# A hybrid diffusion block on one core: a hand-written scan order with its stores issued later and its loads earlier

## The chip, the cores and the metric

The kernel runs on one core of a Trainium2 chip. The metric is the device time of one execution in microseconds. "Before" is the kernel without the change. All line numbers are those of the kernel before. A few words used throughout: PE is TensorE, DVE is VectorE, ACT is ScalarE, POOL is GpSimd, and SP is SyncE, which computes nothing here and issues almost all transfers. Each engine takes its instructions in the order in which they were written for it.

## The reference, cut to what matters

One layer over 2048 latent tokens and 256 context tokens, width 1024, in float32. After a projection, branch A is a gated delta rule that runs over the sequence in both directions and branch B is a gated short convolution; both are projected, gated and merged, multiplied by one more matrix, and added to the input under a layer norm. The change touches the scan of branch A and what is run beside it. Its core is this loop over chunks:

```
def step(s, xs):
    qk_i, q_dec_i, k_dec_i, u_i, w_i, d_i = xs
    v_new = u_i - jnp.einsum('bhck,bhkv->bhcv', w_i, s)
    o = jnp.einsum('bhck,bhkv->bhcv', q_dec_i, s) + jnp.einsum('bhcs,bhsv->bhcv', qk_i, v_new)
    s = s * d_i[..., None, None] + jnp.einsum('bhck,bhcv->bhkv', k_dec_i, v_new)
    return s, o
```

It is run for two directions over the same chunks, and the two outputs are added, then normalised per head and multiplied by a gate:

```
o = o * lax.rsqrt(jnp.mean(o * o, axis=-1, keepdims=True) + RMS_EPS) * w
y = o * jax.nn.silu(z)
merged = jax.nn.sigmoid(g_a) * (y_a @ w_a) + jax.nn.sigmoid(g_b) * (y_b @ w_b)
```

## The kernel before

Three stages follow one another. The projections fill the first half of the time. Then comes the scan (method `window`), and at the end the output product and the layer norm (method `final`). The change lies in the scan and in its helpers.

The scan works in chunks of 128 tokens with all 8 heads in one tile. There are 18 chunks (2 of context, 16 latent) and two directions, so 36 **visits**; forward and backward alternate. Visits 0 to 3 are context. A latent chunk is visited twice, once in each direction. The second visit is marked `again`; visits 20 to 35 are of that kind. A first visit computes two products of keys and queries (`N` and `QK`, method `gram`), multiplies them by the decays and keeps the raw products in HBM. A visit that is `again` loads them from there (`gram_load`, L153) and only multiplies (L160). A first visit stores its output (`od`); an `again` visit loads it (`op`, L1311), adds its own (L1320), normalises the sum (`norm`), and turns and gates it (`norm_out`: load `zat`, transpose on PE, multiply on DVE at L1494, store `yad` at L1495).

The loop is a software pipeline written out by hand: `tc.manual_schedule` keeps the written order on all five engines. Pass `i` of the loop works on four visits at once: `v0` (visit i) updates the state, `v1` inverts its triangular matrix, `v2` forms `QK`, `v3` loads its keys and decays, forms `N` and begins its inverse. The inverse of `v3` is a generator `sol` of 20 small DVE steps (L186 to L215), handed out one or two at a time between the other work by `go(sol, n)`. The decays of `v3` are a generator `dec` of four parts (`visit_decay`). The norm of the visit before is a generator `norms` of five parts.

Beside the scan runs filler work on PE: `dense(n)` takes the next n matmuls of the eight remaining products (jobs b1, b2, b0, b3, then a0 to a3; each job is 8 units `m` of 24 matmuls). Each unit loads its two weight tiles `wh`, `wl` one unit ahead (L361, two buffers), loads a gate tile `gt`, and ends in `evac`: DVE multiplies (L1227), in the a jobs POOL adds `mt` (L1229), and SP stores (L1230). An a job may begin when its four chunks have been normalised (`ready`, `done`); its input `yr` is loaded (L1205) and split by ACT and POOL (L366, L367).

What matters for the change is the one list of transfers that SP goes through in the written order. A store waits there until its data are ready, and all loads written after it wait behind it. Four such places:

- `evac` issues its store right behind the multiplication (L1230);
- `norm_out` issues, for each half of the heads, the load of `zat` (L1490) and then the store of the product (L1495), so that the second load stands behind the first store;
- the kept product `QK` of `v2` is loaded (L1367 calls L153) in the pass in which it is used, a few lines above its use;
- `kT` and the decays `gcb` of `v3` are loaded at the start of the pass in which `visit_decay` begins to work on them; `kT` has three buffers, and the fourth visit's load waits for the product of `v0` with its keys (L320).

Of the kernel before, what the change touches and what calls it, by code (L numbers as in the profile page):

```python
# [15 lines left out]
P = 128  # L16
D = 1024
KT = 8
H = 8
# [18 lines left out]
class Kern:  # L38
    def __init__(self, tc):
        self.tc = tc  # L40
        self.nc = tc.nc
        self.es = ExitStack()
        self.due, self.tick, self.phase_of, self.pending, self.tail = [], 0, {}, [], False

# [52 lines left out]
    def visit_load(self, v):  # L97

        nc, g2 = self.nc, self.g2
        src = v["src"]  # L100
        v["kT"] = self.gk.tile([P, H, P], F32, name="kT", bufs=3)
        nc.sync.dma_start(v["kT"], src["kT"])
        v["gcb"] = self.gb.tile([P, H, P], F32, name="gcb")
        nc.sync.dma_start(v["gcb"].rearrange("p h t -> p (h t)"), src["gc"])
# [15 lines left out]
    def visit_decay(self, v):  # L120
# [20 lines left out]
        for h in range(H):  # L141
            nc.vector.scalar_tensor_tensor(out=gcb[:, h, :], in0=gcb[:, h, :], scalar=gcT[:, h:h + 1], in1=self.mask[d],
                                           op0=ALU.subtract, op1=ALU.min)
        nc.scalar.activation(out=gcb, in_=gcb, func=AF.Exp)
# [1044 lines left out]
    def window(self, es, settle):  # L1189
# [36 lines left out]
        def evac(job, m, ps, gt, mt):  # L1226
            nc.vector.scalar_tensor_tensor(out=gt, in0=gt, scalar=1.0, in1=ps, op0=ALU.add, op1=ALU.mult)  # L1227
            if job[0] == "a":
                (nc.vector if self.tail else nc.gpsimd).tensor_tensor(out=gt, in0=gt, in1=mt, op=ALU.add)  # L1229
            nc.sync.dma_start((self.mb_d if job[0] == "b" else self.mg_d)[job[1]][m], gt)  # L1230
# [15 lines left out]
        def fillers():  # L1246
# [3 lines left out]
            for jn, job in enumerate(jobs):  # L1250
# [17 lines left out]
                for m in range(8):  # L1268
# [3 lines left out]
                    if m < 7:  # L1272
                        w.append(self.load_w(W, m + 1))
                    elif nxt is not None and ready(nxt):
                        fed = True
                        w.append(self.load_w("w_b" if nxt[0] == "b" else "w_a", 0))
                        if nxt[0] == "a":
                            for k in range(KT):
                                fetch(nxt, k)
# [61 lines left out]
        with tc.manual_schedule(engines={ET.PE, ET.DVE, ET.Activation, ET.Pool, ET.SP}):  # L1341
# [6 lines left out]
            def turn():  # L1348
                for n, parts in turned:
                    self.norm_out(n, parts)  # L1350
                    done.add(n)
                turned.clear()

            for i in range(-3, nv):
                get = lambda k: vs[i + k] if 0 <= i + k < nv else None
                v0, v1, v2, v3 = get(0), get(1), get(2), get(3)
                dec = self.visit_decay(v3) if v3 else iter(())
                if i < -1:
# [5 lines left out]
                if v3:  # L1364
                    self.visit_load(v3)
                    self.gram_load(v3, "N")
                if v2 and v2["latent"]:  # L1367
                    self.gram_load(v2, "QK")
# [10 lines left out]
                if v3:  # L1379
                    self.visit_load_q(v3)  # L1380
                go(sol, 2)
                if v1:
                    self.inv_d16(v1)
                go(sol)
# [8 lines left out]
                if i >= -1:  # L1393
                    dense(4)
                go(sol, 2)
# [9 lines left out]
                if v0:  # L1405
                    self.st_o(v0, 1)
                if late:
# [7 lines left out]
                if v0:  # L1415
                    self.st_u(v0, 1)
                if v1:
                    self.inv_d32(v1)
                go(dec)
                go(norms)  # L1420
                go(sol, 9)
# [13 lines left out]
                if i == -1 or v3 and v3["again"] or not v3:  # L1435
                    dense(8)
                if v1:
# [5 lines left out]
                go(sol)  # L1443
            go(norms, 9)
            turn()
            return fil
# [15 lines left out]
    def norm(self, n, parts):  # L1462
# [3 lines left out]
        ms = g2.tile([P, H], F32, name="ms")  # L1466
        for hs, o in parts:
# [15 lines left out]
    def norm_out(self, n, parts):  # L1483
# [4 lines left out]
        for hs, o in parts:  # L1488
            za = g1.tile([P, 4, P], F32, name="zat", bufs=2)
            nc.sync.dma_start(za, self.za_d[n // 4][n % 4][:, hs, :])  # L1490
# [4 lines left out]
            nc.sync.dma_start(self.ya_d[gi][hs, :, sl].rearrange("h p t -> p h t"), za)  # L1495
# [225 lines left out]
```

## Time and profile before

| | |
|---|---|
| time, median of 2 runs | 3618.56 us (3615.84 to 3621.28) |
| profiled execution, its own time | 3615.66 us |
| its span, first to last instruction | 3613.9 us |
| busy, share of the span | PE 84%, DVE 62%, ACT 42%, POOL 39% |
| PE clock granted, mean | 0.910 of full speed |
| projections | 0 to 1855 us |
| scan, start (passes -3 to 0) | 1855 to 1967 us |
| scan, first visits (passes 1 to 17) | 1967 to 2473 us |
| scan, passes 18 to 34 | 2473 to 3238 us |
| last pass and norms | 3238 to 3297 us |
| rest of the fillers, output product, layer norm | 3297 to 3614 us |

Read it so: PE is the busiest engine over the whole span, but the whole span is a mean over stages that have different limits. 17 passes with first visits take 506 us; the 17 passes after them, in which a visit is `again`, take 765 us.

### The profile page before, as it was taken

Reading aid. Unit: us, or ns where it says so; the run is one execution under the profiler, and the core shown is the slowest. Engines: PE = TensorE matmul, PEld = TensorE weight load, DVE = VectorE, ACT = ScalarE, POOL = GpSimd, SP = SyncE. Lnnn points to the kernel's source line nnn. Section 1 sums busy time; section 2 is a strip of 40 time slices with the busy share of each in tenths; the row PEclk is TensorE's granted clock in tenths of the full one; section 3 lists DMA queues with packets and bytes.
Section 4 is the critical chain, followed back from the end, with each engine's and each line's share of the span. In section 5 each row is a group of like instructions: output and inputs, shape, how many; then the busy total and the mean of one; then the engine's idle time right before and its main releaser. Section 6 shows DMA issues by size and latency. Waiting matters only on the chain. (4 is left out here: it accounts for less than half of the span.)

```text
span 3613.9 us, 60210 instructions
## 1 busy us (share of the span) xinstructions
PE 3033.2 (84%) x22089; PEld 2499.0 (69%) x22089; DVE 2237.2 (62%) x5658; ACT 1516.8 (42%) x3405; POOL 1395.4 (39%) x1021
## 2 busy tenths in 40 slices
PE   7899899999989999999977888887665555577788
PEld 4677688888867778887865777776554545465576
DVE  7657555556566656564226777876665555544499
ACT  4654543334465543333413555554443334332121
POOL 3544467666665546666610111111102112103264
PEclk9999999999999999999988898998877777788899
DMA  5535753235643322233355556566444444356742
GB/s 202 142 95 153 220 161 105 77 117 172 193 143 111 95 66 83 83 97 113 101 176 211 182 194 240 199 225 227 148 155 170 176 152 160 129 174 219 244 155 105
DMA packets 405380, 557.23 MB, mean 154 GB/s; under 512 B 28244, under 2 KB 278613, under 8 KB 404060
## 3 DMA queue, kind: packets, MB, share of 16 engines
q1 hardware_dynamic: 382158, 520.77, 44.1%
q10 hardware_dynamic: 22926, 32.62, 2.5%
q8 instruction: 173, 2.83, 0.3%
q14 instruction: 123, 1.01, 0.1%
HBM read 391.66 MB, written 161.64 MB: 153 GB/s over the span
## 5 line engine op out<-in xcount | busy, mean ns | idle before, releaser
L783 PE MATMUL pd<-bh,ah 128*128 128x512 f32 x2240 | 892.9, 399 | 10.4 <-ACT u L803 5.8
L785 PE MATMUL pd<-bh,al 128*128 128x512 f32 x2240 | 880.2, 393 | 0.0
L784 PE MATMUL pd<-bl,ah 128*128 128x512 f32 x2240 | 880.0, 393 | 0.0
L367 POOL TENSOR_TENSOR al<-s,ah 128x512 fp32r<-128x512 f32 x348 | 479.0, 1380 | 470.0 <-ACT ah L366 447.0
L367 POOL TENSOR_TENSOR al<-raw,ah 128x512 fp32r<-128x512 f32 x260 | 370.2, 1428 | 320.7 <-ACT ah L366 285.2
L783 PEld LDWEIGHTS pd<-bh,ah 128*128 128x128 f32 x2240 | 425.2, 190 | 98.9 <-issue 6.5
L785 PEld LDWEIGHTS pd<-bh,al 128*128 128x128 f32 x2240 | 424.8, 190 | 90.5 <-POOL al L367 0.3
L784 PEld LDWEIGHTS pd<-bl,ah 128*128 128x128 f32 x2240 | 425.4, 190 | 85.2
L118 POOL TENSOR_TENSOR kt<-kt,kd 128x1024 f32<-128x1024 f32 x36 | 68.4, 1901 | 842.9 <-DMA kt<-kd 574.2
L366 ACT CAST ah<-s 128x512 fp32r<-128x512 f32 x352 | 214.1, 618 | 292.4 <-PE pd L784 268.5
L366 ACT CAST ah<-raw 128x512 fp32r<-128x512 f32 x264 | 162.3, 616 | 260.7 <-PE pd L784 169.4
L1282 PE MATMUL pf<-ah,wh 128*128 128x512 f32 x512 | 227.1, 444 | 49.3 <-DMA wh<-w_bhd 17.2
L340 PE MATMUL pst<-S,qd 128*128 128x128 f32 x512 | 122.1, 327 | 151.3 <-DVE ot L1320 139.4
L769 DVE TENSOR_TENSOR s<-s,raw 128x512 f32<-128x512 f32 x80 | 110.7, 1383 | 220.0 <-POOL s L769 220.0
L1286 PE MATMUL pf<-ah,wl 128*128 128x512 f32 x512 | 230.2, 450 | 18.2 <-DMA wl<-w_ald 16.7
L1284 PE MATMUL pf<-al,wh 128*128 128x512 f32 x512 | 223.7, 437 | 2.7 <-POOL al L367 2.6
L340 PEld LDWEIGHTS pst<-S,qd 128*128 128x128 f32 x512 | 97.4, 232 | 157.4 <-DVE ot L1320 141.5
L208 DVE TENSOR_TENSOR R<-R,rb 128x120 f32<-128x120 f32 (+4 forms) x540 | 189.3, 350 | 1.2
L205 DVE TENSOR_TENSOR rb<-rb,R 128x120 f32<-128x120 f32 (+4 forms) x540 | 166.8, 309 | 14.2
L1282 PEld LDWEIGHTS pf<-ah,wh 128*128 128x128 f32 x512 | 110.0, 215 | 74.0 <-issue 30.4
L146 POOL TENSOR_TENSOR qd<-qd,qT 128x1024 f32<-128x1024 f32 x32 | 75.6, 2363 | 215.0 <-ACT qd L138 128.2
L308 PE MATMUL pinv<-r,w 64*64 64x64 f32 x576 | 57.2, 272 | 113.2 <-ACT w L297 113.2
(349 smaller groups left out, 6011.6 us busy)
## 6 DMA issues: line engine op xcount, KB each, us to landing
raw<-in_w_in SPq DMA_DIRECT2D x160, 512.0 KB
kT<-kTd SPq DMA_DIRECT2D x36, 512.0 KB
gcb<-gcd SPq DMA_DIRECT2D x36, 512.0 KB
kt<-kd SPq DMA_DIRECT2D x36, 512.0 KB
vh<-vd SPq DMA_DIRECT2D x36, 512.0 KB
wh<-w_bhd SPq DMA_DIRECT2D x32, 512.0 KB
wl<-w_bld SPq DMA_DIRECT2D x32, 512.0 KB
qT<-qTd SPq DMA_DIRECT2D x32, 512.0 KB
```

The costliest lines, as they stand in the source:

```text
L205: nc.vector.tensor_tensor(out=t, in0=t, in1=bc(R[:, :, j:j + 1], c.stop - c.start), op=ALU.mult)
L208: nc.vector.tensor_tensor(out=R[:, :, c], in0=R[:, :, c], in1=t, op=ALU.add)
L340: nc.tensor.matmul(po[:, j, :], v["qd"][:, h, :], S[:, h, :], start=True, stop=False)
L366: self.nc.scalar.copy(out=hi, in_=src)
L367: (eng or self.nc.gpsimd).tensor_tensor(out=lo, in0=src, in1=hi.bitcast(F32), op=ALU.subtract)
L769: eng.tensor_tensor(out=o, in0=a, in1=b, op=op)
L783: mm(ps, hi[:, k, :], bh, start=(first and k == 0), stop=False, skip_group_check=not first)
L784: mm(ps, hi[:, k, :], bl, start=False, stop=False, skip_group_check=not first)
L785: mm(ps, lo[:, k, :], bh, start=False, stop=(last and k == 3), skip_group_check=not first)
L1282: mm(ps, wh[:, k, :], ah, start=(k == 0), stop=False)
L1284: mm(ps, wh[:, k, :], al, start=False, stop=False)
L1286: mm(ps, wl[:, k, :], ah, start=False, stop=(k == KT - 1))
```

## The change

1. **Stores behind their data.** `evac` and `norm_out` no longer issue their stores; they put them on a list `hold`. A new function `ship`, called five times in a pass, issues what the call before it took from `hold`. So a store is issued between one and two fifths of a pass behind the instruction that makes its data, in the written order. The mark that a chunk is done (`done.add`) goes through the same list, behind its store. In the first two passes (`early`) and in the last stage (`tail`) stores are issued at once, as before.
2. **Keys and decays one visit ahead.** `visit_load` (kT, gcb) is called for `v4` in the middle of the pass, no longer for `v3` at its start; `kT` gets a fourth buffer. The load of `qT` moves a few lines down.
3. **Kept product `QK` ahead.** It is loaded for `v3` late in the pass (behind `st_o(v0, 1)`), no longer for `v2` at the start of the next one.
4. **`zat` ahead.** Both halves are loaded when the norm begins, one pass before `norm_out`.
5. **Decays in five parts.** The eight DVE instructions (L142) are a part by themselves, in front of `inv_d32`; the ACT exponential (L144) and the POOL product (L146) follow two `sol` steps later.
6. **`sol`** has its last steps behind `inv_w64`, and one step fewer at the end of the pass.
7. **Input of the next a job** is asked for (`yr`, and whether the job is ready) one unit earlier, at m = 6; the weights as before at m = 7.

```
+        self.hold, self.early = [], True
...
-        v["kT"] = self.gk.tile([P, H, P], F32, name="kT", bufs=3)
+        v["kT"] = self.gk.tile([P, H, P], F32, name="kT", bufs=4)
...
                                            op0=ALU.subtract, op1=ALU.min)
+        yield
         nc.scalar.activation(out=gcb, in_=gcb, func=AF.Exp)
...
-            nc.sync.dma_start((self.mb_d if job[0] == "b" else self.mg_d)[job[1]][m], gt)
+            put = lambda: nc.sync.dma_start((self.mb_d if job[0] == "b" else self.mg_d)[job[1]][m], gt)
+            put() if self.tail or self.early else self.hold.append(put)
...
-                    elif nxt is not None and ready(nxt):
+                    elif fed:
+                        w.append(self.load_w("w_b" if nxt[0] == "b" else "w_a", 0))
+                    if m == 6 and nxt is not None and ready(nxt):
                         fed = True
-                        w.append(self.load_w("w_b" if nxt[0] == "b" else "w_a", 0))
...
                     self.norm_out(n, parts)
-                    done.add(n)
+                    self.hold.append(lambda n=n: done.add(n))
...
+            shelf = []
+            def ship(all=False):
+                for fn in shelf + (self.hold if all else []):
+                    fn()
+                shelf[:] = [] if all else self.hold
+                self.hold.clear()
+            self.visit_load(vs[0])
             for i in range(-3, nv):
...
+                self.early = i < -1
...
                 if v3:
-                    self.visit_load(v3)
                     self.gram_load(v3, "N")
-                if v2 and v2["latent"]:
-                    self.gram_load(v2, "QK")
...
                     dense(8)
-                if v3:
-                    self.visit_load_q(v3)
+                ship()
                 go(sol, 2)
                 if v1:
                     self.inv_d16(v1)
+                if v3:
+                    self.visit_load_q(v3)
+                if v4:
+                    self.visit_load(v4)
...
                     dense(4)
+                ship()
...
                     self.st_o(v0, 1)
+                if v3 and v3["latent"]:
+                    self.gram_load(v3, "QK")
+                ship()
...
                     self.st_u(v0, 1)
+                go(dec)
                 if v1:
                     self.inv_d32(v1)
+                ship()
+                go(norms)
+                go(sol, 2)
                 go(dec)
-                go(norms)
-                go(sol, 9)
...
                     dense(8)
+                ship()
                 if v1:
                     self.inv_d64(v1)
...
-                go(sol)
+            ship()
+            ship(True)
             go(norms, 9)
             turn()
+            ship(True)
...
         ms = g2.tile([P, H], F32, name="ms")
+        self.za = [g1.tile([P, 4, P], F32, name="zat", bufs=2) for _ in parts]
+        for (hs, _), za in zip(parts, self.za):
+            nc.sync.dma_start(za, self.za_d[n // 4][n % 4][:, hs, :])
...
-        for hs, o in parts:
-            za = g1.tile([P, 4, P], F32, name="zat", bufs=2)
-            nc.sync.dma_start(za, self.za_d[n // 4][n % 4][:, hs, :])
+        for (hs, o), za in zip(parts, self.za):
...
-            nc.sync.dma_start(self.ya_d[gi][hs, :, sl].rearrange("h p t -> p h t"), za)
+            self.hold.append(lambda hs=hs, za=za: nc.sync.dma_start(self.ya_d[gi][hs, :, sl].rearrange("h p t -> p h t"), za))
```

## Rows read from the trace of the kernel before

**Rows 1.** Busy time of each engine by stage: us, then busy us.

```profile
core 0: us, PE busy (x) PEld busy (x) DVE busy (x) ACT busy (x) POOL busy (x), PEclk, DMA share, GB/s
...
1967.00:2473.00 506.00, 430.80 (x6219) 381.64 (x6210) 395.88 (x1642) 265.99 (x553) 76.45 (x51) 0.91 0.58 209
2473.00:3238.00 765.00, 467.42 (x6054) 412.18 (x6053) 453.05 (x1784) 292.60 (x810) 108.83 (x77) 0.76 0.46 161
3238.00:3297.00 59.00, 40.64 (x184) 32.57 (x184) 17.91 (x40) 14.62 (x44) 12.65 (x10) 0.83 0.56 186
```

**Rows 2.** Timeline of SP's issues: start, us, line, transfer.

```profile
2473.89 0.32 SPq L102 DMA_DIRECT2D kT<-kTd  x1
...
2622.81 0.42 SPq L153 DMA_DIRECT2D QK<-kqd  x1
...
2637.48 0.37 SPq L1495 DMA_DIRECT2D yad<-zat  x1
2637.89 0.50 SPq L1490 DMA_DIRECT2D zat<-zad  x1
...
3238.24 0.86 SPq L1311 DMA_DIRECT2D op<-od  x2
```

**Rows 3.** DVE's waits, 2473 to 3238: total us, times, longest.

```profile
DVE QK L160 <- DMA QK<-kqd: 88.4, 16, 12.0
DVE zat L1494 <- DMA zat<-zad: 84.3, 18, 10.1
DVE r32t L215 <- ACT r L212: 44.7, 16, 3.0
DVE n L186 <- ACT n L184: 41.4, 16, 11.4
DVE ot L1320 <- PE pst L341: 18.6, 15, 2.8
DVE S L353 <- PE pst L348: 11.3, 5, 6.1
DVE zat L1494 <- issue: 3.8, 1, 3.8
```

**Rows 4.** PE's waits, 2473 to 3238.

```profile
PE pst L340 <- DVE ot L1320: 135.2, 15, 18.1
PE pinv L267 <- DVE r32t L243: 80.9, 14, 11.3
PE pinv L308 <- ACT w L297: 54.4, 13, 14.7
PE pinv L239 <- ACT w L230: 20.8, 12, 3.8
```

**Rows 5.** Timeline of DVE in one pass; brackets: idle before, and releaser.

```profile
2630.64 1.23 DVE L160 TENSOR_TENSOR QK<-QK,gcb 128x1024 f32<-128x1024 f32 x1 [3.19 <-DMA QK<-kqd]
...
2632.42 1.99 DVE L205 TENSOR_TENSOR rb<-rb,R 128x96 f32<-128x96 f32 x1
...
2634.50 0.24 DVE L208 TENSOR_TENSOR R<-R,rb 128x96 f32<-128x96 f32 x1
...
2641.14 0.75 DVE L1494 SCALAR_TENSOR_TENSOR zat<-gram,cvT,zat 128x512 f32<-128x512 f32 x1 [3.69 <-DMA zat<-zad]
```

**Rows 6.** The chain that ended last: one weight load, start and us.

```profile
3284.38 5.75 DMA wl<-w_ald
```

**Rows 7.** ACT's waits for the next a job's input, 2446 to 3297.

```profile
ACT ah L366 <- DMA yr<-yad: 24.6, 2, 13.3
```

**Rows 8.** PE's waits, 1967 to 2473.

```profile
PE pinv L308 <- ACT w L297: 55.1, 17, 7.1
```

**Rows 9.** DVE's waits, 1967 to 2473.

```profile
DVE t L129 <- DMA gcb<-gcd: 25.9, 14, 5.7
DVE n L186 <- ACT n L184: 25.8, 17, 1.8
```

**Rows 10.** Timeline of POOL in the same pass as Rows 5.

```profile
2632.40 1.90 POOL L118 TENSOR_TENSOR kt<-kt,kd 128x1024 f32<-128x1024 f32 x1 [24.00 <-DMA kt<-kd]
```

More of the change, by code (lines that the diff above doesn't have):

```diff
@@ L1350, in turn @@
                     self.norm_out(n, parts)
-                    done.add(n)
+                    self.hold.append(lambda n=n: done.add(n))
                 turned.clear()
+            shelf = []
[5 more added lines that the diff above has]
+            self.visit_load(vs[0])
             for i in range(-3, nv):
                 get = lambda k: vs[i + k] if 0 <= i + k < nv else None
-                v0, v1, v2, v3 = get(0), get(1), get(2), get(3)
+                v0, v1, v2, v3, v4 = (get(k) for k in range(5))
                 dec = self.visit_decay(v3) if v3 else iter(())
+                self.early = i < -1
                 if i < -1:
```

## The prediction

> **What bounds the kernel now.** I read the busy time by stage first [rows 1]. The mean over the span says that PE is the busiest engine, but the change touches only the scan. In the 17 passes from 1967 to 2473 PE is busy 430.8 of 506 us: 85%, and nearly its own bound. In the 17 passes from 2473 to 3238 (the issues at 2473.89 and 3238.24 open passes 18 and 35 [rows 2]) PE is busy 467 of 765 us, DVE 453, and no engine is over 61%. One pass takes 45.0 us there against 29.8 us before. That stretch is the place to look at.
>
> Next, who waits in it. DVE's waits [rows 3] add up to 292 us for the seven rows; with its 453 us of work that is 745 of 765 us. So DVE is always either working or in one of a few named waits: its list of instructions, waits included, sets the pace, and each wait that goes shortens it one for one until another engine's list is as long. PE's two longest waits [rows 4] are for DVE (`ot`, `r32t`), that is, for instructions queued behind DVE's own waits; they are echoes.
>
> Then why DVE waits. 88.4 us are for `QK`, 88.1 us for `zat` (84.3 and the 3.8 that the view calls issue). The timeline of one pass shows both: `QK` is asked for at 2622.81 and DVE stands 3.19 us before it at 2630.64; the second `zat` is asked for at 2637.89, right behind the store of the first at 2637.48, and DVE stands 3.69 us [rows 2, 5]. DVE makes the data, SP stores them, only then does SP ask for what DVE needs next. In passes that also store a gate product the first `zat` and `QK` come later still (10.1 and 12.0 us at most [rows 3]).
>
> **The change part by part.** First the 17 passes from 2473 to 3238.
>
> `QK` ahead: the same 16 loads, asked for about half a pass before the use. The 88.4 us go. The load now stands behind `st_o(v0, 1)`, whose QK buffer it takes over, so SP waits there for PE. Queued behind it on SP are one set of stores, the `zat` loads of this norm (used a pass later), and gate and weight loads of a unit that begins within the next 24 matmuls. Nothing there is needed at once: 0 us, and up to the 5.75 us of a weight load [rows 6] in a pass where a unit begins just then.
>
> `zat` ahead: 34 loads asked for a pass early, 88.1 us go. The load must wait until the buffer's last store, issued a few lines above, has landed; it has most of a pass for that: 0 us.
>
> The `sol` step at the end of the pass moved behind the state product's DVE work: now DVE multiplies `vh` (eight instructions) while ACT makes `n16`, where it used to wait. 41.4 us for 16 passes, the longest 11.4 [rows 3]. That one lies behind ACT's wait for a late job input, one of two that make 24.6 us [rows 7]; taken whole, since that wait goes too (part 7 of the change).
>
> The other DVE waits I leave: `r32t` 44.7, `ot` 18.6, `S` 11.3 us. `r32t` could fall, since the exponential (L144) no longer stands with the squares before the `r32` products on ACT, or rise, since these products now stand behind the copy of `w64`: from -44.7 to +44.7 us (a second wait as long); taken 0.
>
> Stores behind their data: SP's waits at stores vanish from the path. The number of stores is the same, and what they gave DVE to wait for is in the sums above already.
>
> So DVE's list becomes 765 - 88.4 - 88.1 - 41.4 = 547 us, 32.2 a pass. What is late next? PE: 467 us busy, and its waits for ACT, 54.4 and 20.8 us [rows 4], that this change does not remove: 542 us. Two lists of the same length, coupled at some six places in a pass, do not both run full. The passes from 1967 show how much is lost: there PE is the fullest at 85% [rows 1], and 467 / 0.85 is 550. I take the larger of the two, and 5% for the coupling: 575 us, that is **190 us gained**. Bounds: 100 (PE's echoes turn out half real) and 245 (r32t gone, PE's clock up).
>
> PE's clock belongs to this: the granted clock was 0.76 here and 0.91 in the passes before [rows 1], a mix of the levels of 1.2 and 2.4 GHz. It is lower where PE waits more. If the waits go, PE's 467 us should shrink; this is the reason why I let DVE and not PE be the bound.
>
> The passes 1 to 17: PE is the bound, so only its own 75 us of idle time can be won. 55.1 us of that are one wait of 3 us a pass, `inv_d64` for ACT's copy of `w64` [rows 8]. That copy stands behind the exponential of the decays, which waits for DVE, and DVE is behind by its waits for `gcb` and `n`, 25.9 and 25.8 us [rows 9]. Both go: `gcb` is asked for a pass earlier, `n` is covered as above. 51.7 us off DVE's list, passed on to a wait of 55.1; the fill-up of PE takes some: **30 us**, with bounds of 0 and 55. New on SP: the load of `gcb` for `v4` has two buffers and must wait for DVE's `QK` of the same pass; qT, the first stores and any unit's loads are queued near it, with most of a pass to spare.
>
> The last pass, 3238 to 3297: ACT stands up to 13.3 us for the input of the next a job [rows 7], and what needs ACT on PE and DVE stands with it. Asked for a unit earlier, it is there: **15 us** with the zat loads, bounds 5 and 22.
>
> Start: the first keys and decays are asked for before the first filler's loads and not behind them: **3 us**, bounds -3 and 10.
>
> What costs. `done` is marked two ships later. Counting both written orders through, the fillers that run in the scan are 1160 instead of 1164, so four matmuls of 128x512 move into the last stage: under 2 us, kept in the range. The fourth `kT` buffer is memory only.
>
> Sum: 190 + 30 + 15 + 3 = 238 us. From the profiled 3615.7 us that is 3378; the median of the runs shown is 3 us above the profile, so **3380 us**. Two per cent, 72 us, is about what a measurement of this kernel can tell from no change.
>
> A rule to set against this. The row: DVE's small product L205 took 1.99 us at 2632.42, while a product of that shape took 0.24 us at 2634.50, and POOL's product ran from 2632.40 for 1.90 us [rows 5, 10]: DVE stood still for as long as POOL worked. The Trainium skill (GPSIMD Engine Reference, Key points) says that POOL shares its SBUF interfaces with VectorE and contends with DVE instructions that have two SBUF inputs. The trace agrees. It speaks against the change: while DVE waited, POOL's work cost nothing, and a DVE that never waits pays for all of it. It is the third rival.
>
> **The rivals.**
>
> *PE takes over.* Its waits for DVE are not all echoes: `st_o` needs its PSUM bank and its own place in the order. If half of the 135.2 us before L340 stays [rows 4], PE's list is 467 + 54 + 21 + 68 = 610 us, and with 5% for coupling 640: 125 us gained in place of 190, and 10 in place of 30 in the passes before: 3465. For it: both lists come out within 5 us of each other. Against it: in the timeline that wait ends with `ot`, directly behind `zat`.
>
> *Everything fits.* The clock rises to that of the passes before, `r32t` goes: 245 + 55 + 22 + 10 = 332 us, 3286.
>
> *POOL's work is paid in full.* POOL is busy 108.8 us in the 17 passes [rows 1]. Were all of it hidden in DVE's waits now, DVE's list would be 547 + 109 = 656, 690 with coupling: 75 gained in place of 190, so 3495. Against it: of the key product the row shows that it is paid already [rows 5].
>
> *Nothing is gained.* "A fifth of a pass" is written order, not time. If SP runs ahead of the engines it still reaches each store before its data, waits, and the loads behind it are as late as now. Then the time stays within 2%: 3590. Against it: the two loads that count are moved to a place a whole pass or half a pass ahead, so a wait of some microseconds at a store no longer reaches their users.
>
> *SP becomes the bound (slower).* The order ties SP to two engines in every pass: to DVE's `QK` through the two `gcb` buffers, and to PE's `st_o(v0, 1)` through the three `QK` buffers. Every weight load behind these two points starts later. A unit lasts 24 matmuls, three quarters of a pass, 22 us of a pass of 29.8; a weight load takes 5.75 us [rows 6]. It decides from the point at which SP is held for more than 16 us a pass: from there PE stands for the weights, 5.75 us in each of 35 passes, 201 us, and if half of the gains go with it (119), 3615.7 - 119 + 201 = 3700. Against it: `QK` is multiplied within 10 us of the start of a pass, and after that SP waits for nothing but PE itself.
>
> **How the numbers follow.** Forecast 0.52; PE takes over 0.22; everything fits 0.08; POOL in full 0.08; nothing gained 0.06; slower 0.04. The first four are all faster by over 2%: 0.90. Range: the distances of the four terms to their bounds, added in squares (90, 30, 10, 6 us downwards in gain; 55, 25, 7, 7 upwards), give 3318 to 3476 around the forecast; extended a little towards *everything fits* and to nearly all of *POOL in full*: 3300 to 3490, which also holds *PE takes over*.
>
> **What would show it.** In the profile after, for passes 18 to 34: the rows `QK <- DMA` and `zat <- DMA` gone or under 10 us; `n <- ACT` gone; a pass of 33 to 35 us; DVE busy over 75%; PE's clock over 0.80; L340's wait for `ot` under half. In passes 1 to 17, the wait of `inv_d64` under 30 us. The transition of jobs without ACT's wait for `yr`. The projections and the last 317 us as before. I am wrong if DVE's waits come back under another name (`r32t`, `gcb`, `S`), if PE waits for `wh` or `wl` in the scan, or if SP shows long waits for `st_o` with loads behind that someone stands for.

## The result, and the profile after

The changed kernel takes 3282.74 us (median of 2 runs, 3277.4 to 3288.09) against 3618.56: a ratio of 0.907, 95% interval 0.900 to 0.914. It is faster, as forecast, but by 336 us and not by 238; 3283 lies 17 us below the range of 3300 to 3490. The profiled execution took 3288.09 us, its span is 3286.4.

From here on the span is cut at DVE's first multiplication of `vh` in a pass (L322, in the changed kernel L324), the same event in every kernel. First the windows by stage of the changed kernel, cut at passes 3, 18 and 35:

```profile
core 0: us, PE busy (x) PEld busy (x) DVE busy (x) ACT busy (x) POOL busy (x), PEclk, DMA share, GB/s
2002.50:2414.90 412.40, 372.69 (x5576) 331.99 (x5562) 338.89 (x1471) 236.88 (x492) 67.47 (x45) 0.96 0.65 237
2414.90:2935.10 520.20, 428.50 (x6063) 376.17 (x6063) 453.16 (x1785) 298.00 (x823) 113.63 (x77) 0.88 0.69 236
2935.10:3286.40 351.30, 287.01 (x1180) 225.26 (x1178) 256.11 (x332) 74.81 (x154) 159.46 (x104) 0.91 0.56 189
```

And the kernel before at the same cuts, in place of the round ones of [rows 1]:

```profile
2025.90:2473.50 447.60, 386.94 (x5600) 343.17 (x5598) 354.26 (x1470) 236.95 (x491) 67.48 (x45) 0.93 0.60 213
2473.50:3240.90 767.40, 469.81 (x6069) 414.24 (x6069) 452.61 (x1784) 295.47 (x819) 108.83 (x77) 0.76 0.46 162
3240.90:3613.90 373.00, 293.91 (x1176) 230.91 (x1174) 256.86 (x331) 74.82 (x154) 159.17 (x104) 0.89 0.55 183
```

The reader is to see three things. The gain is 23.4 us up to pass 3, 35.2 in passes 3 to 17, 247.2 in passes 18 to 34 and 21.7 behind them, together the 327.5 us between the spans. In passes 18 to 34 DVE's work is the same 453 us, but fills 87% of the time in place of 59%. And PE does the same work there, 6063 matmuls against 6069, in 428.5 us of busy time in place of 469.8, at a granted clock of 0.88 in place of 0.76.

DVE's waits of the changed kernel in passes 18 to 34, which answer to [rows 3] (total us, times, longest):

```profile
DVE r32t L217 <- ACT r L214: 23.4, 12, 13.5
DVE ot L1324 <- PE pst L343: 9.9, 10, 1.7
DVE zat L1519 <- PE gram L1518: 3.9, 6, 1.6
...
DVE S L355 <- PE pst L350: 1.3, 2, 1.1
```

PE's waits in the same passes, which answer to [rows 4]:

```profile
PE pinv L241 <- ACT w L232: 43.2, 14, 4.6
PE pinv L310 <- ACT w L299: 22.2, 14, 4.6
PE pf L1286 <- ACT ah L368: 13.6, 1, 13.6
PE pst L342 <- DVE ot L1324: 5.5, 4, 2.3
```

No wait for `QK`, for the load of `zat` or for `n` is left, and what DVE still waits for (`r32t`, `ot`, `S`) is less than half of what it was. PE's 135.2 us before `st_o` are 5.5 and its 80.9 for `r32t` are gone: they were echoes, as the prediction said. Its two waits for ACT, 54.4 and 20.8 us [rows 4], have changed sizes, 22.2 and 43.2. SP's issues of one pass, which answer to [rows 2]:

```profile
2572.71 0.32 SPq L155 DMA_DIRECT2D QK<-kqd  x1
2573.12 0.94 SPq L1520 DMA_DIRECT2D yad<-zat  x2
2577.90 2.27 SPq L1493 DMA_DIRECT2D zat<-zad  x2
```

DVE uses them in the next pass (compare [rows 5]; there are no brackets, so no idle time):

```profile
2591.51 1.22 DVE L162 TENSOR_TENSOR QK<-QK,gcb 128x1024 f32<-128x1024 f32 x1
...
2595.97 1.41 DVE L1519 SCALAR_TENSOR_TENSOR zat<-gram,cvT,zat 128x512 f32<-128x512 f32 x2
```

Both loads now have 18 us. In passes 3 to 17 two of DVE's waits count; of [rows 9] neither is left:

```profile
DVE r32t L217 <- ACT r L214: 43.6, 15, 3.0
DVE QK L173 <- ACT zat L171: 16.1, 10, 2.3
```

and PE's wait at `inv_d64` is shorter, first before and then after, both in passes 3 to 17 ([rows 8] has two passes more):

```profile
PE pinv L308 <- ACT w L297: 43.5, 15, 5.7
PE pinv L310 <- ACT w L299: 25.9, 14, 4.1
```

### The profile page after: what moved, and what is told of

Read it like the earlier page. It is cut to its first block, busy times and chain, and to the rows that moved or that the text cites. A ratio compares the mean times of both kernels' runs of the same rounds, so it can differ in the third digit from the quotient of the medians.

```text
span 3286.4 us, 60301 instructions
## 1 busy us (share of the span) xinstructions
PE 2963.1 (90%) x22089; PEld 2436.8 (74%) x22089; DVE 2212.4 (67%) x5658; ACT 1517.6 (46%) x3405; POOL 1401.0 (43%) x1021
## 5 line engine op out<-in xcount | busy, mean ns | idle before, releaser
L1286 PE MATMUL pf<-ah,wh 128*128 128x512 f32 x512 | 219.1, 428 | 48.5 <-DMA wh<-w_bhd 21.9
L1290 PE MATMUL pf<-ah,wl 128*128 128x512 f32 x512 | 221.4, 432 | 20.0 <-DMA wl<-w_ald 17.4
L1288 PE MATMUL pf<-al,wh 128*128 128x512 f32 x512 | 216.4, 423 | 0.6 <-POOL al L369 0.6
L207 DVE TENSOR_TENSOR rb<-rb,R 128x120 f32<-128x120 f32 (+4 forms) x540 | 165.2, 306 | 14.2
L210 DVE TENSOR_TENSOR R<-R,rb 128x120 f32<-128x120 f32 (+4 forms) x540 | 159.7, 296 | 1.2
L1290 PEld LDWEIGHTS pf<-ah,wl 128*128 128x128 f32 x512 | 103.9, 203 | 48.1 <-DMA wl<-w_ald 22.9
L1047 ACT ACTIVATE t<-t 128x512 f32<-128x512 f32 (+1 forms) x112 | 67.2, 600 | 141.2 <-DVE t L1032 141.1
L342 PE MATMUL pst<-S,qd 128*128 128x128 f32 x512 | 105.4, 288 | 17.5 <-ACT v L334 9.6
```

The lines of the kernel that those rows point to most:

```text
L207: nc.vector.tensor_tensor(out=t, in0=t, in1=bc(R[:, :, j:j + 1], c.stop - c.start), op=ALU.mult)
L210: nc.vector.tensor_tensor(out=R[:, :, c], in0=R[:, :, c], in1=t, op=ALU.add)
L342: nc.tensor.matmul(po[:, j, :], v["qd"][:, h, :], S[:, h, :], start=True, stop=False)
L1286: mm(ps, wh[:, k, :], ah, start=(k == 0), stop=False)
L1288: mm(ps, wh[:, k, :], al, start=False, stop=False)
L1290: mm(ps, wl[:, k, :], ah, start=False, stop=(k == KT - 1))
```

## The experiments

Kernels named a_ put parts of the change on the kernel before, u_ undo parts in the changed kernel, t_ add work to it, b_ try to better it; each was timed beside the kernel before. The theory at the start: DVE's two late loads were the stall of passes 18 to 34 and had to be asked for earlier, the held stores cost and give nothing, the new order gives about 41 us there, and DVE now sets the pace. Rivals: the held stores carry the gain (A), the order does (B), PE sets the pace now (C). The table gives the median, the ratio to the kernel before with its 95% interval, and the length of the four stretches in the profiled execution of each (up to pass 3; passes 3 to 17; 18 to 34; the rest). Stretches differ between kernels that are alike there (passes 18 to 34 take 518.7 us in u_yr and 512.1 in u_kt): under some 10 us in one stretch decides nothing. And each row's stretches are those of one execution, which can lie off the median: 17 us above it in t_pe, 10 above in b_pool, 10 below in a_hold.

| kernel | us | ratio | to 3 | 3-17 | 18-34 | rest |
|---|---|---|---|---|---|---|
| before | 3618.6 | 1 | 2025.9 | 447.6 | 767.4 | 373.0 |
| changed | 3282.7 | 0.907 [0.900, 0.914] | 2002.5 | 412.4 | 520.2 | 351.3 |
| a_qkzat | 3435.2 | 0.949 [0.947, 0.951] | 2024.2 | 443.1 | 604.1 | 360.9 |
| a_ord | 3588.2 | 0.992 [0.989, 0.994] | 2025.9 | 460.7 | 729.5 | 372.7 |
| a_qkzat_ord | 3390.7 | 0.936 [0.934, 0.937] | 2028.5 | 454.6 | 550.3 | 359.9 |
| a_all_loads | 3360.2 | 0.928 [0.925, 0.930] | 2000.7 | 421.7 | 570.1 | 358.2 |
| a_hold | 3446.6 | 0.953 [0.952, 0.955] | 2019.9 | 434.1 | 630.6 | 350.6 |
| u_hold | 3298.6 | 0.912 [0.910, 0.914] | 2006.3 | 414.1 | 525.4 | 351.6 |
| u_ord | 3344.8 | 0.924 [0.921, 0.926] | 2005.5 | 425.7 | 565.7 | 352.2 |
| u_kt | 3303.8 | 0.913 [0.910, 0.915] | 2020.0 | 418.4 | 512.1 | 349.4 |
| u_yr | 3286.8 | 0.908 [0.905, 0.910] | 2005.9 | 410.9 | 518.7 | 347.7 |
| u_qk | 3275.1 | 0.905 [0.904, 0.907] | 2000.4 | 412.4 | 505.9 | 350.3 |
| u_zat | 3295.8 | 0.911 [0.908, 0.913] | 2003.3 | 411.0 | 522.7 | 354.4 |
| u_qkzat | 3292.9 | 0.911 [0.909, 0.913] | 2001.9 | 410.7 | 518.8 | 353.1 |
| t_dve | 3327.1 | 0.918 [0.916, 0.920] | 2012.0 | 430.2 | 536.4 | 347.8 |
| t_pe | 3319.4 | 0.917 [0.914, 0.920] | 2012.5 | 447.0 | 525.1 | 350.0 |
| b_r32 | 3297.2 | 0.910 [0.908, 0.912] | 2007.6 | 434.6 | 510.8 | 350.9 |
| b_yield | 3281.3 | 0.906 [0.904, 0.908] | 2007.2 | 411.3 | 511.1 | 348.6 |
| b_pool | 3292.7 | 0.910 [0.908, 0.912] | 2007.0 | 415.7 | 525.2 | 352.9 |
| b_best | 3273.7 | 0.905 [0.903, 0.906] | 2000.5 | 412.1 | 508.8 | 350.7 |

**a_qkzat, the two loads alone.** On the kernel before:

```
-                if v2 and v2["latent"]:
-                    self.gram_load(v2, "QK")
...
                     self.st_o(v0, 1)
+                if v3 and v3["latent"]:
+                    self.gram_load(v3, "QK")
...
         ms = g2.tile([P, H], F32, name="ms")
+        self.za = [g1.tile([P, 4, P], F32, name="zat", bufs=2) for _ in parts]
+        for (hs, _), za in zip(parts, self.za):
+            nc.sync.dma_start(za, self.za_d[n // 4][n % 4][:, hs, :])
```

(and the load taken out of `norm_out`).

> The kernel before with two things changed: QK asked for half a pass ahead, zat a whole pass ahead; stores, other loads and the order of the inverse stay. Theory (late loads of DVE's inputs were the stall): the 88 us of QK and 88 us of zat in passes 18 to 34 go, so about 3440 us, down to 3410 if the waits for r32t, ot and S shrink with them; nothing in passes 1 to 17. Rival A (the held stores are what matters, since SP stands at a store before it reaches the moved loads): under 60 us gained, over 3555, with QK and zat still waited for. Rival B (the new order of the inverse is what matters): under 80 us gained, and the waits come back under n or r32t.

Measured: 3435.2. Passes 18 to 34 fall by 163.3 us, against 176.5 in the sum. DVE's waits there:

```profile
DVE r32t L215 <- ACT r L212: 44.7, 16, 3.0
DVE n L186 <- ACT n L184: 43.7, 15, 11.4
DVE t L129 <- DMA gcb<-gcd: 17.0, 5, 5.5
```

`QK` and `zat` are gone, `r32t` and `n` stand as before, and a wait for `gcb` comes up that [rows 3] does not have. Rivals A and B are not needed for this much; whether A could do as much is a_hold's question, below.

**a_ord, the new order alone.** On the kernel before:

```
                 if v1:
+                go(dec)
+                if v1:
                     self.inv_d32(v1)
-                go(dec)
                 go(norms)
-                go(sol, 9)
+                go(sol, 2)
+                go(dec)
...
-                go(sol)
             go(norms, 9)
```

with the extra `yield` ahead of the exponential in `visit_decay`.

> The kernel before with the new order of inverse and decays alone (decays in one more part, one inverse step moved behind the state product). Theory: about 41 us in passes 18 to 34 (the n wait) and 25 in passes 1 to 17, so 3550, between 3530 and 3590; QK and zat are waited for as before (about 88 us each). Rival B (the order is what matters): 150 us or more, 3465 or less. Rival A: under 40.

Measured: 3588.2; 37.9 us less in passes 18 to 34, 13.1 us more in passes 3 to 17. DVE's waits in passes 18 to 34:

```profile
DVE QK L161 <- DMA QK<-kqd: 110.1, 16, 13.9
DVE zat L1495 <- DMA zat<-zad: 81.3, 18, 9.5
DVE r32t L216 <- ACT r L213: 20.3, 13, 9.8
```

The `n` wait is gone and that for `r32t` halved, but 22 us of it come back at `QK`. In passes 3 to 17, where DVE had waited for `n`, it now waits for the next late thing:

```profile
DVE t L129 <- DMA gcb<-gcd: 49.2, 15, 5.2
DVE r32t L216 <- ACT r L213: 41.6, 15, 3.0
```

They were 19.2 and 21.3 us in the same passes of the kernel before. So with a late `gcb` the order loses there; in the changed kernel, where `gcb` is in time, it gains (u_ord, below).

**u_hold, the stores at once.** In the changed kernel the three `self.hold.append(...)` became direct calls:

```
-            put() if self.tail or self.early else self.hold.append(put)
+            put()
```

> The changed kernel with every store issued right behind its data again, all loads still ahead. Theory: the loads have half a pass or more to spare, so SP standing at a store costs nothing: within 30 us of the changed kernel, 3283 to 3313. Rival A (the held stores carry the gain): over 3400, with QK, zat or gcb waited for again by DVE.

Measured: 3298.6, 16 us above the changed kernel; passes 18 to 34 at 525.4. None of DVE's waits for `QK`, `gcb` or the load of `zat` is back there. With all loads early, the place of the stores makes no difference that the intervals (0.910 to 0.914, and 0.900 to 0.914) can tell.

**u_ord, the old order in the changed kernel** (a_ord's diff backwards).

> The changed kernel with the old order of inverse and decays. Theory: the wait for n comes back, 41 us in passes 18 to 34 and some 25 in passes 1 to 17: 3330 to 3350. Rival B (order carries the gain): over 3430. If it costs nothing (under 20 us), n was an echo of the late job input and of the late loads, and the order did no work.

Measured: 3344.8. The order is worth 45.5 us in passes 18 to 34 and 13.3 in passes 3 to 17, and nothing else takes its place.

**u_kt, keys and decays late again.** In the changed kernel:

```
-        v["kT"] = self.gk.tile([P, H, P], F32, name="kT", bufs=4)
+        v["kT"] = self.gk.tile([P, H, P], F32, name="kT", bufs=3)
...
                 if v3:
+                    self.visit_load(v3)
                     self.gram_load(v3, "N")
```

without the two early calls.

> The changed kernel with keys and decays asked for at the start of the pass that uses them again (three key buffers). Theory (the early gcb load is what ended DVE's gcb wait and the late start): 15 to 20 us come back before pass 3, some 25 us in passes 3 to 17, little (under 15) in passes 18 to 34: 3320 to 3345. Rival (the early load of gcb also carries the rest of the gain in passes 18 to 34 that the moved QK and zat loads alone left open, 84 us): 3380 or more, with gcb waits of DVE in those passes. If nothing comes back, this part of the change did no work.

Measured: 3303.8, less than expected. The start loses 17.5 us and passes 3 to 17 six, where 25 were expected; passes 18 to 34 lose nothing, and DVE has no wait for `gcb` there. DVE's wait for the decays between 1850 and 2020 is

```profile
DVE t L130 <- DMA gcb<-gcd: 27.7, 5, 19.3
```

against this of the changed kernel from 1850 to pass 3:

```profile
DVE t L130 <- DMA gcb<-gcd: 16.1, 1, 16.1
```

**u_yr, the next job's input asked for one unit later**, as in the kernel before:

```
-                    if m == 6 and nxt is not None and ready(nxt):
+                    elif nxt is not None and ready(nxt):
                         fed = True
```

> The changed kernel with the input of the next job asked for in the last unit again and not in the last but one. Theory: ACT waits for yr again as in the kernel before, some 10 us at each of the four job changes: 5 to 20 us longer, 3290 to 3305, on the passes with a job change and on pass 35. Rival: the gain at the end of the scan (22 us) comes from elsewhere: no difference, 3283.

Measured: 3286.8, no difference, and pass 35 and what follows took 347.7 us. The rival holds: this part did no work.

**t_dve and t_pe, more work on one engine.** In the changed kernel, with the same result:

```
+        for _ in range(6):
             nc.vector.tensor_tensor(out=n16, in0=n16, in1=rows(self.tri16[d]), op=ALU.mult)
```

```
-        for h in range(H):
+        for h in list(range(H)) * 3:
             nc.tensor.matmul(dp[p1, h, :], v["w64"][p2, h, :], v["r64"][p2, h, :], start=True, stop=True)
```

> The changed kernel with 2.5 us more of DVE's work in every pass (the product with the 0/1 triangle, 0.495 us, made six times in place of once; the result is the same), in 34 passes. Theory (DVE's list sets the pace of passes 18 to 34, PE that of passes 3 to 17): passes 18 to 34 grow by 0.8 to 1.0 of 2.5 us each, 32 to 42 us in all; passes 3 to 17 by under 15 us: 3318 to 3340. Rival C (PE sets the pace everywhere): under 15 us in passes 18 to 34, 3283 to 3300.

> The changed kernel with 2.5 us more of PE's work in every pass (the eight matmuls of inv_d64, 80 ns each of new issue, made three times in place of once; the result is the same). Theory (DVE sets the pace of passes 18 to 34, PE that of passes 3 to 17): passes 3 to 17 grow by 0.8 to 1.0 of 2.5 us, 28 to 36 us; passes 18 to 34 by under 15 us: 3313 to 3335. Rival C (PE everywhere): 32 to 42 us in passes 18 to 34 as well, 3345 to 3365.

Measured: 3327.1 and 3319.4. The windows of passes 3 to 17 and 18 to 34, first with more for DVE:

```profile
2012.00:2442.20 430.20, 382.38 (x5599) 340.19 (x5599) 367.49 (x1544) 236.57 (x491) 67.58 (x45) 0.94 0.64 228
2442.20:2978.70 536.50, 425.19 (x6065) 372.64 (x6064) 474.58 (x1866) 299.78 (x823) 112.75 (x77) 0.90 0.66 228
```

then with more for PE:

```profile
2012.50:2459.50 447.00, 422.72 (x6074) 382.67 (x6073) 344.29 (x1470) 237.30 (x489) 68.37 (x46) 0.90 0.62 218
2459.50:2984.60 525.10, 459.35 (x6614) 406.74 (x6614) 445.38 (x1784) 298.05 (x822) 110.40 (x77) 0.90 0.68 234
```

The added product took less than planned: DVE's busy time grew by 21.4 us in passes 18 to 34, and the time by 16.2, three quarters of it. PE's grew by 30.9 there and the time by 4.9, one sixth, though t_pe's profiled execution is 17 us over its median. So DVE rather than PE sets the pace in those passes, and rival C falls; each engine was loaded at one place of the pass only, and three quarters is a little under the 0.8 that the theory had. In passes 3 to 17 the time grew by 17.8 of DVE's 28.6 and by 34.6 of PE's 50.0: both lists are on the path there, which neither theory had.

**a_qkzat_ord and a_all_loads**, on the kernel before: the diffs of a_qkzat and a_ord together; and all loads ahead (a_qkzat and the early keys and decays), with order and stores as before.

> The kernel before with QK and zat ahead and the new order of inverse and decays; stores at once, keys and decays loaded as before. Theory (parts add, but in passes 3 to 17 the new order lays bare the late gcb): passes 18 to 34 take 604 - 38 = 566 us, passes 3 to 17 some 13 more than the kernel before, 460, since gcb is waited for again: 3400 to 3415. Rival D (the order is worth more once the loads are early): passes 18 to 34 at 520 to 540, 3370 to 3385. If they stand at 566, the 46 us to the changed kernel's 520 belong to early gcb or held stores.

> The kernel before with all loads ahead (keys, decays, QK, zat); order and stores as before. Theory: as with QK and zat alone, less the gcb waits of DVE (14.8 and 17.4 us in the two stretches there) and some 20 us before pass 3: passes 18 to 34 some 590 us, passes 3 to 17 some 430: 3375 to 3395. Rival A (stores at once hold SP up, so the early gcb load gives nothing): 3410 or more.

Measured: 3390.7 and 3360.2, both below what was expected. With QK, zat and the order, passes 18 to 34 take 550.3 us, 217.1 less than before. DVE's waits there:

```profile
DVE t L129 <- DMA gcb<-gcd: 26.6, 6, 6.4
DVE r32t L216 <- ACT r L213: 20.4, 13, 9.9
```

What is missing to the changed kernel's 520.2 is 30.1 us, and the wait for `gcb`, which nothing else covers now, is 26.6. All loads early (570.1) lack the order: `n` and `r32t` are waited for as before.

**u_qk, u_zat and u_qkzat, the early loads undone in the changed kernel**, one and both (a_qkzat's diff backwards).

> The changed kernel with QK asked for at the start of the pass that uses it. Theory (QK by itself stalls DVE as in the kernel before, 88 us in passes 18 to 34): 55 to 90 us come back: 3338 to 3373. Rival E (the stall came from what stood ahead of QK on SP, which now issues its stores later): under 25 us, 3283 to 3307.

> The changed kernel with zat asked for in the same pass as its use. Theory: 88 us of the kernel before come back at least in part; the second load no longer stands behind the store of the first, so one wait in a pass, not two: 40 to 85 us, 3323 to 3368. Rival E (only the store ahead of the second load cost time): under 25 us, 3283 to 3307.

> The changed kernel with QK and zat both asked for as late as before; held stores, early keys and decays and the new order stay. Theory F: what the single undoings cost, -8 and +13 us: 3280 to 3305. Theory as first stated: each covers for the other, and both undone cost 100 us or more: 3380 and up.

Measured: 3275.1, 3295.8 and 3292.9. The theory as I had put it falls: the two loads that gave 184 us by themselves cost nothing measurable when taken back, one by one (8 us less and 13 more) or together (10 more). `zat` is waited for again, but 17.6 us in u_zat and 18.8 in u_qkzat, not 88.1; `QK` is not. SP's issues in u_qk show why:

```profile
2613.35 0.32 SPq L155 DMA_DIRECT2D N<-kkd  x1
2613.72 0.42 SPq L155 DMA_DIRECT2D QK<-kqd  x1
```

DVE multiplies at

```profile
2624.28 1.22 DVE L162 TENSOR_TENSOR QK<-QK,gcb 128x1024 f32<-128x1024 f32 x1
```

The load stands where it stood before, but SP comes to it 10.6 us ahead of the use, against 7.8 us in [rows 2, 5] with 3.19 of them as a wait. What had been late was SP, not the place of the load. In the three kernels the keys still have their fourth buffer and are asked for early, so it need not be the held stores alone that let SP come sooner (see a_hold).

**a_hold, the held stores alone**, on the kernel before; no load moved.

> The kernel before with held stores alone; no load moved ahead, order as before. Theory F (QK and zat came late only because SP stood at a store whose data was not made yet; either a later store or an earlier load removes it): most of the 184 us that the early loads gave, 120 to 190: 3430 to 3500, with SP's long waits at the stores of zat and of the gate products gone. Theory as first stated (the loads must be asked for earlier): under 60 us, over 3560, with the QK wait still near 88 us.

Measured: 3446.6, 170 us gained with no load asked for earlier in the written order. DVE's waits in passes 18 to 34:

```profile
DVE r32t L216 <- ACT r L213: 44.3, 16, 3.1
DVE QK L161 <- DMA QK<-kqd: 37.6, 14, 5.6
...
DVE zat L1514 <- DMA zat<-zad: 11.4, 4, 4.3
```

`QK` has fallen from 88.4 to 37.6, `zat` from 88.1 to 11.4. SP's waits in the kernel before, in the same passes, are the reason:

```profile
SPq L1495 <- DVE zat L1494: 152.4, 19, 14.3
SPq L1230 <- POOL R L190: 102.6, 5, 22.4
SPq L102 <- PE pst L320: 93.7, 10, 19.4
SPq L1230 <- POOL gt L1229: 76.6, 9, 17.4
SPq L1230 <- DVE gt L1227: 60.4, 4, 23.2
```

Four of the lines are stores (of `zat` and of gate products), 392 us of standing with loads behind them. Theory F holds: a later store and an earlier load are two ways out of one queue.

The line of L102 is a load, that of `kT`, which stands until one of its three buffers is free; `QK` is loaded a few lines behind it. With held stores alone SP stands there longer:

```profile
SPq L103 <- PE pst L321: 160.7, 15, 15.3
```

The 37.6 us that DVE still waits for `QK` in a_hold fit this line: in u_qk and u_qkzat, where the keys come early and have four buffers, the load of `QK` is as late in the order and DVE has no wait for it. So the keys share in the remedy when `QK` is loaded late. No run separates their part from that of the stores.

**b_r32, b_yield and b_best, attempts at a faster kernel.** In the changed kernel:

```
-                go(sol, 2)
+                go(sol, 3)
                 go(dec)
```

```
                     if not self.tail:
                         yield True
+                        yield True
```

and both, the first with `3 if v2 and v2["again"] else 2`.

> The changed kernel with the ACT products of r32 one step earlier in the order (ahead of the exponential of the decays and the copy of w64), an attempt at a faster kernel. If DVE's wait for r32t (23 us in passes 18 to 34, 44 in passes 3 to 17) is on the path, most of it goes: 3240 to 3260. If PE's wait for w64 (22 and 26 us) grows by as much, since that copy now stands behind the recursion: 3283 or longer, up to 3310.

> The changed kernel with one more step between the request of a late job's input and its use on ACT, an attempt at a faster kernel. In passes 24 and 30 (42.7 and 36.6 us, their neighbours 30.5) ACT stands 6.2 us for yr and PE 13.6, DVE 13.5 behind it: 10 to 18 us go there, and 4 to 8 matmuls move into the last stage at twice (up to 3 us): 3268 to 3276. Rival: the order of ACT, not the load, makes the long passes: no gain, 3283 to 3290.

> The changed kernel with one more step for a late job's input, and the ACT products of r32 one step earlier in the passes with kept products alone, where that attempt gained 9 us (elsewhere it lost 22): passes 18 to 34 at 500 to 507 us in place of 520, passes 3 to 17 unchanged at 411 to 414: 3262 to 3275. Rival: both gains are the same 9 us (the wait for r32t behind the late input), 3272 to 3282.

Measured: 3297.2, 3281.3 and 3273.7. The earlier `r32` loses 22.2 us in passes 3 to 17; in passes 18 to 34 it is 9.4 us below. In passes 3 to 17 DVE's wait for `r32t` falls from 43.6 to 12.3, but PE waits longer for the copy of `w64`, which now stands behind the recursion:

```profile
PE pinv L310 <- ACT w L299: 43.1, 15, 5.4
```

It was 25.9, and DVE's wait for PE at `vh` (L324) grew from 1.8 to 32.7. With one more step for the late input passes 18 to 34 are 9.1 us below, and with both 11.4, not the sum of 18.5, as the rival had it. These are at the limit of what a stretch can tell, and the ratio of b_best, 0.905, lies within the changed kernel's interval (so does that of u_qk): a faster version is not shown.

**b_pool, one product moved from DVE to POOL:**

```
-            nc.vector.tensor_tensor(out=N, in0=N, in1=v["gcb"], op=ALU.mult)
+            (nc.gpsimd if name == "QK" else nc.vector).tensor_tensor(out=N, in0=N, in1=v["gcb"], op=ALU.mult)
```

> The changed kernel with the product QK by the decays (1.22 us on DVE, 16 times in passes 18 to 34) on POOL. If DVE's list sets the pace there: 19.5 us less for DVE, of which 0.4 to 0.75 (as the test with more DVE work showed) are gained: 3268 to 3275. If POOL's longer product (2.1 to 2.4 us by its other products of that size) stands in DVE's way, or the first matmul with QK waits for it: 3283 to 3300.

Measured: 3292.7, no gain. The window of passes 18 to 34:

```profile
2422.70:2947.90 525.20, 429.69 (x6003) 377.61 (x6000) 464.72 (x1770) 298.21 (x823) 148.72 (x93) 0.89 0.68 233
```

DVE lost 16 products (19.5 us) and is busy 464.7 us, 11.6 more than in the changed kernel. The group of its recursion that updates `R` in b_pool,

```profile
L210 DVE TENSOR_TENSOR R<-R,rb 128x120 f32<-128x120 f32 (+14 forms) x240 | 78.9, 329 | 0.6
```

and in the changed kernel,

```profile
L210 DVE TENSOR_TENSOR R<-R,rb 128x120 f32<-128x120 f32 (+14 forms) x240 | 62.8, 262 | 0.6
```

shows where: the same 240 instructions are 16.1 us longer. Another 11.0 us are in the 16 products with the triangle (L189), 495 ns each in the changed kernel and 1180 here. All of DVE's other work grew by 31.1 us while POOL's 16 products took 39.2 us.

## Why the prediction was wrong in size

The sum of the gains was 238 us, and the spans differ by 327.5. Of the 89.5 us between, 57.2 are in passes 18 to 34 (190 forecast, 247.2 measured), 20.4 before pass 3, 6.7 at the end and 5.2 in the first visits.

**The direction and most of the mechanism were right.** The waits for `QK`, `zat` and `n` went, DVE sets the pace of passes 18 to 34, PE's waits for DVE were echoes, and its clock rose. Of the list of signs, the pass of 33 to 35 us failed (it is 30.6), and a job's input is still late once (6.2 us on ACT). One argument did not carry what was put on it: that DVE's work and its waits add up to the stretch. The same holds of PE in the kernel before, 467 us of work and 298 of waits in 765, so the sum picks no engine. What does is for whom each waits: PE for DVE, and DVE for transfers.

**Passes 18 to 34, the step that failed.** The 190 us were 217.9 us of waits less 28 us: 547 us were raised to 575 by taking PE's list of 550 and "5% for the coupling". a_qkzat_ord aims at just these three waits and gains 217.1 us, so there was nothing to subtract on the whole. That it agrees with the 217.9 to 1 us is luck in part: DVE's waits for `r32t` and `ot` also fell, from 63.3 us to 27.5, and a wait of 26.6 us for `gcb` and some small ones came up. PE's list did not stand in the way. It was computed with the busy time of the old clock, which fell by 41 us, as the text itself said it should, yet the 550 us kept it; and its two waits for ACT, said to stay at 75 us, are 65.4. The second miss is 30.1 us for the early decays and the held stores, costed at zero in this stretch. The wait for `gcb` was not among the rows of before because DVE came to it late; it came up as soon as the others were gone (17.0 us in a_qkzat, 26.6 in a_qkzat_ord), and either the held stores (u_kt) or the early load (u_hold) is enough to remove it. The three waits that were left as they stood, 74.6 us [rows 3], are 34.6: `r32t` fell with the order alone, to 20.3, where the prediction had named a cause for a fall and one for a rise and set the term to zero (which instruction on ACT made the difference was not traced); `ot` fell with the loads alone (8.7).

**The stores.** "What they gave DVE to wait for is in the sums above already" was right: nothing adds up twice. But the held stores were taken to give nothing of their own, and the late loads to be cured only by asking earlier. Early loads alone gain 163.3 us there, held stores alone 136.8, and in the changed kernel either the stores (16 us) or the loads of `QK` and `zat` (8 us less to 13 more) can be taken back at a cost within the intervals. What has no substitute among the parts is the order, 45.5 us.

**Passes 1 to 17 and the start.** 30 and 3 us were forecast, 35.2 (from pass 3) and 23.4 measured. For the 30, `gcb` and `n` went as said, but the wait for `r32t` doubled, from 21.3 to 43.6 us, and PE alone is not the bound there (t_dve). The start, with bounds of -3 and 10, was looked at by its first load only; DVE waited for `gcb` five times before pass 3, 35.1 us in all, and u_kt gives 17.5 us back.

**The last pass.** 15 us were forecast and 21.7 measured, but not by the step named: u_yr takes the earlier input back at no cost. Held stores alone bring that stretch to 350.6, the loads alone to 360.9. Which transfer it was in the last passes was not traced further.

**The rivals.** "Everything fits" (3286, a chance of 0.08) gave the time to 4 us, with the clock up and the waits for `r32t` halved. Its terms are right for passes 18 to 34 (245 us) and for the end (22); that the whole fits is luck in part, since 55 us for the first visits (35.2 measured) and 10 for the start (23.4) make up for one another. "PE takes over" fell with t_pe. SP does wait in the changed kernel, 113.9 us for `st_o` and 62.3 for the QK product, but no one waits behind it for weights in passes 18 to 34. "POOL's work is paid in full" was nearly right as a mechanism (below) and wrong as a term: DVE's busy time had held this cost before the change as well, 453 us in both kernels.

## What to carry to other kernels

A load that comes late on an in-order queue has two causes that look alike, its own place and what stands ahead of it; look at what the issuing engine waited for before moving the load, and expect the remedies to replace one another, not to add. In this kernel the sum of the removed waits came out at its face value, without a deduction for coupling, but it hid a wait that those waits had covered, so look for what becomes late next. That work and waits of an engine fill a stretch does not yet make it the one that sets the pace; extra work on one engine at a time tells. And if the clock is expected to rise, the list of the engine that it drives is to be computed with the risen clock.

## What was not expected of the hardware

In b_pool POOL's added products cost DVE most of their length: 39.2 us of them made DVE's other instructions 31.1 us longer. 27.1 of these are in two groups with two inputs in SBUF (L210, 262 to 329 ns, and L189, 495 to 1180 ns), though not every such group is longer (L207 went from 356 to 344 ns); the shuffles of the same recursion (L200), with one input, stayed at 222 and 223 ns. The Trainium skill (GPSIMD Engine Reference, Key points) has POOL's SBUF interfaces shared with VectorE, in contention with instructions of two SBUF inputs; this trace agrees in L210 and L189. So moving this product from DVE to POOL gained nothing, though POOL was busy for only 28% of passes 18 to 34.

PE's busy time is no constant of the work: 6069 and 6063 matmuls took 469.8 us at a granted clock of 0.76 and 428.5 at 0.88, a mix of the levels of 1.2 and 2.4 GHz; with only some of the waits gone the clock was 0.78 (a_ord), 0.81 (a_hold) and 0.83 (a_qkzat), and the busy time still 461 to 462 us.
